# A ring of two buffers for the modulation's dots, and converted weights in four buffers instead of five

## The chip, the cores and the metric

The kernel runs on one core of one Trainium2 chip. The metric is the device time of one execution in microseconds, the median of several runs. The engines are named as in the profile: PE is TensorE (matmuls), PEld its weight loads, DVE is VectorE, ACT is ScalarE, POOL is GpSimd, and SP is the engine that issues most DMAs.

## The reference

Two layers of a decoder trunk, over 512 positions of 1024 features, in float32. Each layer is

```
mod = silu(c) @ w_ada + b_ada                 # six vectors of 1024: sh1, sc1, g1, sh2, sc2, g2
h = rmsnorm(x, norm1_w) * (1 + sc1) + sh1
u = h @ w_in                                  # pooling, convolution, q, k, v, gate logits
merged = sum of sigmoid(gate_i) * (mixer_i(u) @ p_i) over pooling, convolution, attention
x = x + g1 * (merged @ w_out)
h2 = rmsnorm(x, norm2_w) * (1 + sc2) + sh2
x = x + g2 * ((silu(h2 @ w_gate) * (h2 @ w_up)) @ w_down)
```

The vectors of `mod` depend on `c` alone, not on `x`; each can be made at any time before its use.

## The kernel before

**Numbers.** [...] Each operand is split in a high part (`whi` for weights) and a low part (`wlo`, the rest), and `mm3` adds high×high, high×low and low×high.

**Weights.** They come in 312 chunks of up to eight blocks of 128 × 128, in the order in which PE uses them. A chunk goes through three steps. SP fetches it (`fetch`, L232) into one of three `raw` buffers. ACT copies it to `whi` (L325, in `split_w`). DVE subtracts to get `wlo` (L328). `whi` and `wlo` have five buffers each, so the copy of a chunk waits until PE has ended the last matmul on the chunk that is five earlier. `next_w` (L349) asks for as many chunks as `ahead_now` says to be on their way beyond the one that it hands out: 4 in most phases, 3 in the gates' phase, and 2 in the last columns of the phases with a norm behind them, where the call gives the number itself. [...] The DVE part may also be held behind a step of the norm (`hold`).

In the gate and up projections most columns are done in pairs by a scheme that saves products and needs sums of weights (`Sums`, `GateUp`, `glu_pair`). There a chunk may be a sum, which POOL's DMAs (L254, L256) and DVE (L262, L263) make in tiles of the ring `w4`. Such a pair has seven chunks, with 256 columns to a matmul.

**The modulation.** A vector of 1024 takes eight dots. A dot (`ada_dot`, L374) is one DVE instruction over 128 × 1024 numbers that multiplies a piece of `w_ada` by silu(c) and adds up. Its piece is 512 KB, fetched by SP (L398) right where the dot is written down. The first 16 dots, for the first norm, are done at the start. The other 80 are made in steps (`ada_step`) as tasks in a queue `bulk`. PE's work calls `tick` every few matmuls, which adds `bulk_rate` to a credit of at most 4.0 and runs tasks until it is spent; a dot costs 1.2. So up to four dots are written down together when a phase begins with full credit. They are made in these places:

- the gates' phase, beside attention, which is written as generators and interleaved by hand: G1, SC2, SH2 in layer 0 and SC2, SH2 in layer 1 (L901), with `early=True`, so their pieces take a `raw` buffer
- the output projection: G2 (L1004), in `w4`, which has six buffers
- layer 0's first down projection: SC1 and SH1 of layer 1 (L1126), in `w4`
- layer 1's input projection: G1 (L849), in `w4`

Of the kernel before, what the change touches and what calls it, by code (L numbers as in the profile page):

```python
# [12 lines left out]
F32 = mybir.dt.float32  # L13
F32R = mybir.dt.float32r
# [7 lines left out]
P = 128  # L22
D = 1024
# [18 lines left out]
C_BLOCKS = 8  # L42
# [8 lines left out]
RAW, BIG = 3, 46  # L51
# [6 lines left out]
SH1, SC1, G1, SH2, SC2, G2 = range(6)  # L58
# [19 lines left out]
def hybrid_trunk(ctx, tc, xT, ws, ada, cols, pool_w, qk_w, crow, pos, con, out):  # L78
# [5 lines left out]
    wp = ctx.enter_context(tc.tile_pool(name="wp", bufs=4))  # L84
# [6 lines left out]
    def nm(s):  # L91
        uid[0] += 1
        return f"{s}{uid[0]}"
# [13 lines left out]
    def w4(shape, dt=F32):  # L107
        return work.tile(shape, dt, tag="w4", name=nm("w4"), bufs=6)
# [10 lines left out]
    bulk = deque()  # L119
# [31 lines left out]
    def pin(ins):  # L151
        return tc.keep_in_program_order(ins)
# [85 lines left out]
    class Sums:  # L238
# [19 lines left out]
        def first(self):  # L258
            raw = rawt()
            fetch(raw, self.l, self.blocks(0, 0) + self.blocks(1, 0))  # L260
            flat = raw.rearrange("p (g b) n -> p g (b n)", g=2)
            pin(V.tensor_add(self.s12[:, 1], self.s12[:, 0], flat[:, 0]))  # L262
            pin(V.tensor_add(self.s43[:, 0], self.s12[:, 1], flat[:, 1]))  # L263
            return split_w(raw, C_BLOCKS)

        def sums(self, which):
            t = (self.s12, self.s43)[which]
            return split_w(t.rearrange("p g (b n) -> p (g b) n", n=P), C_BLOCKS)

    class GateUp:  # L270
# [9 lines left out]
        def load(self, sub):  # L280
            if sub < 2:
                return self.pair[sub].first()
            if sub < 6:
                return self.pair[sub % 2].sums(sub // 2 - 1)
            raw = rawt()
            fetch(raw, self.l, self.pair[0].blocks(1, 1) + self.pair[1].blocks(1, 1))
            return split_w(raw, C_BLOCKS)
# [33 lines left out]
        return wp.tile([P, C_BLOCKS, P], F32, tag="raw", name=nm("raw"), bufs=RAW)  # L321

    def split_w(raw, n):
        hi = wp.tile([P, C_BLOCKS, P], F32R, tag="whi", name=nm("whi"), bufs=5)
        A.activation(hi[:, :n], raw[:, :n], AF.Copy)  # L325
        lo = wp.tile([P, C_BLOCKS, P], F32R, tag="wlo", name=nm("wlo"), bufs=5)
        with tc.issue_after(hold[0].ins) if hold[0] is not None else nullcontext():
            ins = V.tensor_sub(lo[:, :n], raw[:, :n], f32(hi)[:, :n])  # L328
        pin(ins)
        return hi, lo  # L330
# [13 lines left out]
        fetch(raw, l, blocks)  # L344
        return split_w(raw, len(blocks))

    ahead_now = [4]

    def next_w(ahead=None):  # L349
        ahead = ahead_now[0] if ahead is None else ahead  # L350
# [21 lines left out]
    def ada_dot(aw, l, part, j):  # L372

        return V.scalar_tensor_tensor(aw, aw, 1.0, csil, op0=ALU.mult, op1=ALU.mult,  # L374
                                      accum_out=mod[l][:, part, j:j + 1])
# [17 lines left out]
        else:  # L393
            A.activation(m, m, AF.Identity, bias=colt[:, 0, C_ADA + part * KT + j:C_ADA + part * KT + j + 1])

    def ada_step(l, part, j, early):
        aw = wp.tile([P, D], F32, tag="raw", name=nm("raw"), bufs=RAW) if early else w4([P, D])
        nc.sync.dma_start(aw, ada[l, part, j])  # L398
        pin(ada_dot(aw, l, part, j))

    def ada_end(l, part):
        m = mod[l][:, part]
        V.tensor_add(m, m, colt[:, l, C_ADA + part * KT:C_ADA + (part + 1) * KT])
        if part in (SC1, SC2):
            fold_scale(l, 0 if part == SC1 else 1, 0, KT)
        if part == G1:
            V.tensor_scalar(m, m, 0.5, None, op0=ALU.mult)

    def ada_tasks(l, parts, early=False):
        out = []  # L410
        for part in parts:
            for j in range(KT):
                out.append((1.2, lambda part=part, j=j: ada_step(l, part, j, early)))
            out.append((0.2, lambda part=part: ada_end(l, part)))
        return out

# [298 lines left out]
    for l in range(L):  # L715
# [118 lines left out]
        for j in range(2):  # L834
# [11 lines left out]
            if j == 1:  # L846
                bulk.append((0, lambda: pool_chain(1, pool1)))

        gains = ada_tasks(l, (G1,)) if l > 0 else []  # L849
        bulk.extend(gains[:4])  # L850
        k_ps = wide()
# [46 lines left out]
        V.tensor_mul(cv[1], pb, cv[1])  # L898
        y_conv.append(split_from(cv[1]))

        bulk.extend(ada_tasks(l, (G1, SC2, SH2)[l:], True))  # L901
        bulk_rate[0] = (0.5, 0.35)[l]
        ahead_now[0] = 3

        def gate():
            g = ps_mm()
# [93 lines left out]
                    hold[0] = nrm.apply(ll, i, k, lo, hi)  # L1000
            return go

        ahead_now[0] = 4
        bulk.extend(ada_tasks(l, (G2,)))  # L1004
        bulk_rate[0] = 0.9
        n2 = Norm()
# [241 lines left out]
```

## Time and profile before

| | |
|---|---|
| median of 3 runs | 1481.39 us (1480.77 to 1481.45) |
| profiled execution | 1480.46 us, span 1478.7 us |
| granted PE clock | 0.999 |
| PE busy | 1456.7 us, 99% |
| DVE busy | 1052.2 us, 71% |
| ACT busy | 666.3 us, 45% |
| dots in `w4` buffers | 56, 1220 ns each |
| dots in `raw` buffers | 40, 1218 ns each |

The 56 include the 16 first ones. The span runs from the first to the last instruction; the rest of an execution's time lies around it. In a row of the timeline stand the start and the duration in us, the engine, the line, the operation, what it writes and reads, how many instructions the row holds, and in brackets the idle time ahead and what ended it. In a row of the waits stand the total in us, the number and the longest.

### The profile page before, as it was taken

The page shows a single profiled execution, that of the slowest core. Times are in us where ns is not written, and L with a number is a line of the kernel's source. Part 1 is how long each engine was busy: PE and PEld are TensorE (multiplying, and loading weights), DVE is VectorE, ACT ScalarE, POOL GpSimd, SP SyncE. Part 2 cuts the span into 40 slices and gives each one's busy share as a digit, 9 for nine tenths or more (in the row PEclk, how much of TensorE's full clock was granted, in tenths as well). Part 3 has the DMA queues.
Part 4 walks back from the last instruction along what each step waited for, and adds up shares of the span by engine and source line. Part 5 has one row for each costly group of instructions (what it writes and reads, how often), then busy time and mean ns, then how long its engine had stood idle before and what let it go on. Part 6 is the DMA issues. An engine that isn't in the chain of part 4 may idle for free.

```text
span 1478.7 us, 21940 instructions
## 1 busy us (share of the span) xinstructions
PE 1456.7 (99%) x8443; PEld 1268.0 (86%) x8443; DVE 1052.2 (71%) x1855; ACT 666.3 (45%) x1138; POOL 105.8 (7%) x157
## 2 busy tenths in 40 slices
PE   8999999999999999999999999999999999999999
PEld 6888787778988998989988877778889889989997
DVE  7976887758686876767666777776586757657672
ACT  4634555443453352535444345455335525434350
POOL 0000000001100211210000000000010102111200
PEclk9999999999999999999999999999999999999999
DMA  9514433365337775744334443333462436637431
GB/s 346 199 73 159 141 136 134 115 227 148 109 114 221 207 190 174 198 113 117 114 109 146 155 143 126 102 114 128 143 193 81 141 114 167 191 89 196 131 105 65
DMA packets 84409, 217.19 MB, mean 147 GB/s; under 512 B 10832, under 2 KB 23760, under 8 KB 84304
## 3 DMA queue, kind: packets, MB, share of 16 engines
q1 hardware_dynamic: 67456, 177.37, 35.2%
q0 software_dynamic: 16128, 37.76, 11.6%
q8 instruction: 66, 1.08, 0.3%
q10 hardware_dynamic: 720, 0.66, 0.1%
q14 instruction: 39, 0.32, 0.1%
HBM read 213.65 MB, written 2.10 MB: 146 GB/s over the span
## 4 chain that ended last, share of the span: by engine, by line
PE 84%; DVE 8%; DMA 3%; ACT 3%; issue 1%; SPq 0%; DVEq 0%; ACTq 0%
PE mm L149 72%; PE pair L149 11%; DMA raw<-in_ws 2%; DVE wlo L328 2%; PE mm L155 1%; ACT whi L325 1%; DMA w<-in_ada 1%; DVE w L374 1%; DVE raw L374 1%; ACT tmp L612 0%; DMA x<-in_xT 0%; ACT tmp L614 0%; DVE big L914 0%; SPq L232 0%; DVE big L929 0%
## 5 line engine op out<-in xcount | busy, mean ns | idle before, releaser
L149 PE MATMUL mm<-big,whi 128*128 128x512 f32 (+1 forms) x4362 | 1083.3, 340 | 5.6 <-DVE tmp L1081 2.5
L149 PEld LDWEIGHTS mm<-big,whi 128*128 128x128 f32 x4362 | 746.0, 190 | 93.6 <-DVE tmp L1081 4.1
L149 PE MATMUL mm<-big,wlo 128*128 128x512 f32 (+1 forms) x2181 | 736.1, 337 | 0.0
L149 PEld LDWEIGHTS mm<-big,wlo 128*128 128x128 f32 x2181 | 413.9, 190 | 44.7
L325 ACT ACTIVATE whi<-raw 128x1024 fp32r<-128x1024 f32 (+2 forms) x240 | 248.8, 1039 | 298.3 <-PE mm L149 231.1
L328 DVE TENSOR_TENSOR wlo<-raw,whi 128x1024 fp32r<-128x1024 f32 (+2 forms) x240 | 284.7, 1193 | 81.9 <-ACT whi L325 81.0
L325 ACT ACTIVATE whi<-w 128x1024 fp32r<-128x1024 f32 x72 | 76.2, 1059 | 147.8 <-PE mm L149 107.7
L954 DVE SCALAR_TENSOR_TENSOR x<-mm,mod,x 128x512 f32<-128x512 f32 (+1 forms) x90 | 62.0, 689 | 101.4 <-PE mm L149 101.3
L254 POOL DMA_DIRECT2D w<-in_ws x72 | 48.5, 683 | 982.1 <-DVE w L374 377.3
L328 DVE TENSOR_TENSOR wlo<-w,whi 128x1024 fp32r<-128x1024 f32 x72 | 86.7, 1220 | 31.0 <-ACT whi L325 30.2
L149 PE MATMUL pair<-whi,big 128*128 128x512 f32 x224 | 76.7, 390 | 0.0
L256 POOL DMA_DIRECT2D w<-in_ws x72 | 64.6, 923 | 153.1 <-DMA w<-in_ws 136.3
L149 PE MATMUL pair<-big,whi 128*128 128x256 f32 (+1 forms) x376 | 74.0, 294 | 0.0
L374 DVE SCALAR_TENSOR_TENSOR w<-w,csil 128x1024 f32<-128x1024 f32 x56 | 66.9, 1220 | 9.5 <-DMA w<-in_ada 9.3
L149 PEld LDWEIGHTS pair<-big,whi 128*128 128x128 f32 x376 | 60.4, 191 | 2.2
L149 PE MATMUL mm<-whi,big 128*128 128x512 f32 x160 | 57.2, 394 | 1.7 <-ACT big L497 1.4
L149 PE MATMUL pair<-big,wlo 128*128 128x256 f32 (+1 forms) x188 | 55.3, 294 | 0.0
L511 DVE TENSOR_TENSOR big<-tmp,big 128x512 fp32r<-128x512 f32 x48 | 33.0, 690 | 24.3 <-ACT big L510 23.4
L149 PEld LDWEIGHTS pair<-whi,big 128*128 128x128 f32 x224 | 42.1, 188 | 8.7
L374 DVE SCALAR_TENSOR_TENSOR raw<-raw,csil 128x1024 f32<-128x1024 f32 x40 | 48.4, 1218 | 1.2 <-DMA raw<-in_ada 1.2
L914 DVE SCALAR_TENSOR_TENSOR big<-big,mm 128x512 f32<-128x512 f32 x48 | 32.6, 682 | 21.5 <-PE mm L149 21.1
L149 PE MATMUL pair<-wlo,big 128*128 128x512 f32 x112 | 43.6, 390 | 0.0
(187 smaller groups left out, 1251.5 us busy)
## 6 DMA issues: line engine op xcount, KB each, us to landing
raw<-in_ws SPq DMA_DIRECT2D x146, 512.0 KB, 3.4
w<-in_ws POOLq DMA_DIRECT2D x144, 256.0 KB, 4.6
w<-in_ada SPq DMA_DIRECT2D x56, 512.0 KB, 5.3
raw<-in_ada SPq DMA_DIRECT2D x40, 512.0 KB, 3.2
raw<-in_ws SPq DMA_DIRECT2D x64, 256.0 KB, 4.2
raw<-in_ws SPq DMA_DIRECT2D x24, 384.0 KB, 3.5
raw<-in_ws SPq DMA_DIRECT2D x16, 448.0 KB, 5.3
raw<-in_ws SPq DMA_DIRECT2D x36, 128.0 KB, 3.0
```

The costliest lines, as they stand in the source:

```text
L149: tc.keep_in_program_order(T.matmul(*a, **k))
L155: tc.keep_in_program_order(T.transpose(*a))
L254: nc.gpsimd.dma_start(dst, self.source(0, 1))
L256: nc.gpsimd.dma_start(dst, self.source(*other), accum_op=ALU.add)
L325: A.activation(hi[:, :n], raw[:, :n], AF.Copy)
L328: ins = V.tensor_sub(lo[:, :n], raw[:, :n], f32(hi)[:, :n])
L374: return V.scalar_tensor_tensor(aw, aw, 1.0, csil, op0=ALU.mult, op1=ALU.mult, accum_out=mod[l][:, part, j:j + 1])
L511: V.tensor_sub(lo, src, f32(hi))
L914: V.scalar_tensor_tensor(sg, sg, 1.0, branch, op0=ALU.add, op1=ALU.mult)
L954: V.scalar_tensor_tensor(x[k][:, lo:hi], src, mod[l][:, part, k:k + 1], x[k][:, lo:hi], op0=ALU.mult, op1=ALU.add)
```

## The change

Three things change together. The room in memory stays the same to the byte: two dot tiles of 4 KB a partition come, and one `whi` and one `wlo` of 4 KB each go.

1. `whi` and `wlo` have four buffers instead of five.
2. `ahead_now` is one less in every phase: 3 instead of 4, and 2 instead of 3 in the gates' phase. The calls of `next_w` that give the number themselves stay.
3. A dot's piece goes to a ring `dot` with two buffers that nothing else uses, in all four places; `early` goes. The fetch of a dot now waits for the dot that is two earlier, and no longer for a weight's conversion or a sum.

```
     def split_w(raw, n):
-        hi = wp.tile([P, C_BLOCKS, P], F32R, tag="whi", name=nm("whi"), bufs=5)
+        hi = wp.tile([P, C_BLOCKS, P], F32R, tag="whi", name=nm("whi"), bufs=4)
         A.activation(hi[:, :n], raw[:, :n], AF.Copy)
-        lo = wp.tile([P, C_BLOCKS, P], F32R, tag="wlo", name=nm("wlo"), bufs=5)
+        lo = wp.tile([P, C_BLOCKS, P], F32R, tag="wlo", name=nm("wlo"), bufs=4)
...
-    ahead_now = [4]
+    ahead_now = [3]
...
-    def ada_step(l, part, j, early):
-        aw = wp.tile([P, D], F32, tag="raw", name=nm("raw"), bufs=RAW) if early else w4([P, D])
+    def ada_step(l, part, j):
+        aw = wp.tile([P, D], F32, tag="dot", name=nm("dot"), bufs=2)
         nc.sync.dma_start(aw, ada[l, part, j])
         pin(ada_dot(aw, l, part, j))
...
-        bulk.extend(ada_tasks(l, (G1, SC2, SH2)[l:], True))
+        bulk.extend(ada_tasks(l, (G1, SC2, SH2)[l:]))
         bulk_rate[0] = (0.5, 0.35)[l]
-        ahead_now[0] = 3
+        ahead_now[0] = 2
...
-        ahead_now[0] = 4
+        ahead_now[0] = 3
         bulk.extend(ada_tasks(l, (G2,)))
         bulk_rate[0] = 0.9
```

The order of PE's instructions is the same in both kernels; on ACT, DVE and SP some conversions, dots and fetches change places.

More of the change, by code (lines that the diff above doesn't have):

```diff
@@ L407, in ada_end, with ada_tasks @@
             V.tensor_scalar(m, m, 0.5, None, op0=ALU.mult)
-    def ada_tasks(l, parts, early=False):
+    def ada_tasks(l, parts):
         out = []
@@ L412, in ada_tasks @@
             for j in range(KT):
-                out.append((1.2, lambda part=part, j=j: ada_step(l, part, j, early)))
+                out.append((1.2, lambda part=part, j=j: ada_step(l, part, j)))
             out.append((0.2, lambda part=part: ada_end(l, part)))
```

## The prediction

> **What bounds the kernel now.** I read the page first, then the waits of TensorE alone, then those of ScalarE (ACT), and at the end the timeline around the places where the modulation's dots run.
>
> ```profile
> span 1478.7 us, 21940 instructions
> ...
> PE 1456.7 (99%) x8443; PEld 1268.0 (86%) x8443; DVE 1052.2 (71%) x1855; ACT 666.3 (45%) x1138; POOL 105.8 (7%) x157
> ...
> w<-in_ada SPq DMA_DIRECT2D x56, 512.0 KB, 5.3
> raw<-in_ada SPq DMA_DIRECT2D x40, 512.0 KB, 3.2
> ```
>
> PE is busy 1456.7 of 1478.7 us, so at most 22 us are idle, and the start of the program has a part of that. The next view lists what TensorE waits for.
>
> ```profile
> PE mm L155 <- DVE tmp L619: 4.7, 5, 1.9
> PE mm L149 <- DVE tmp L1081: 2.5, 8, 0.6
> PE mm L149 <- ACT big L909: 2.4, 1, 2.4
> ```
>
> Columns: total us, number, longest. These are the top three rows. No row of this view names a converted weight (`whi` of L325 or `wlo` of L328): TensorE never waits for weights. The largest rows belong to attention (softmax at L619, the gate's branch at L909). The span can therefore fall only through attention's rows, 4.7 + 2.4 = 7.1 us, and grow wherever a conversion, today early, becomes late.
>
> ```profile
> ACT whi L325 <- PE mm L149: 338.8, 141, 4.6
> ACT whi L325 <- DMA raw<-in_ws: 40.1, 27, 3.8
> ```
>
> These are the first two rows of ACT's waits. The first is the lead: 141 conversions wait until TensorE has finished with the buffer they are to overwrite. The kernel runs as far ahead as its buffers allow. The second is the fault that the dots bring: a weight that has not landed yet, with ACT standing in order behind it.
>
> **The change, part by part.** No work goes or comes: the same conversions, the same 80 dots that are made in steps, the same DMAs. What moves is when each may start.
>
> *One buffer fewer, one chunk less ahead.* In phases 512 columns wide, a chunk of eight blocks is 24 matmuls.
>
> ```profile
> 411.70 0.62 PE L149 MATMUL pair<-big,whi 128*128 128x512 f32 x2
> ...
> 412.38 0.62 PE L149 MATMUL mm<-big,whi 128*128 128x512 f32 x2
> ```
>
> Three matmuls take 412.38 − 411.70 = 0.68 us, so a chunk takes 24 × 0.227 = 5.45 us, and the lead of a conversion falls from four chunks (21.8 us) to three (16.3 us). ACT's and DVE's part of one chunk is under 3 us together (two rows of about 1.06 and 1.22 us, shown below), so I cost this at 0 in the wide phases, from 0 to 0. In the gate/up pairs a matmul has 256 columns:
>
> ```profile
> 490.52 1.22 DVE L328 TENSOR_TENSOR wlo<-raw,whi 128x1024 fp32r<-128x1024 f32 x1
> ...
> 498.45 1.23 DVE L328 TENSOR_TENSOR wlo<-w,whi 128x1024 fp32r<-128x1024 f32 x1 [1.18 <-ACT whi L325]
> ```
>
> ```profile
> 492.92 0.40 PE L149 MATMUL pair<-big,whi 128*128 128x256 f32 x2
> ...
> 494.35 0.40 PE L149 MATMUL pair<-big,whi 128*128 128x256 f32 x2
> ...
> 505.87 0.40 PE L149 MATMUL mm<-big,whi 128*128 128x256 f32 x2
> ```
>
> The first fence is DVE, the second PE. From 492.92 to 494.35 lie 12 matmuls, 0.12 us each, so a chunk is 2.88 us. The `wlo` that ends at 499.68 is first used at 505.87, a slack of 6.2 us, which falls by one chunk (2.9) to 3.3: still no wait, so I take 0 in the steady pairs. The upper end is a slack used up in every one of the 18 pairs (72 sums at four a pair), by 0.3 us each, +5.4; I leave that to a rival. The first pair is tighter: the `wlo` that starts at 490.52 ends at 491.74 and is used at 494.35, 2.6 us. That place is costed with the dots.
>
> In the second norm the same cut moves one `wlo` out of the row of three that DVE does just ahead of the norm's apply, to the place of the next row:
>
> ```profile
> 411.55 2.69 DVE L328 TENSOR_TENSOR wlo<-raw,whi 128x768 fp32r<-128x768 f32 x3
> ...
> 401.82 0.39 PE L149 MATMUL mm<-big,whi 128*128 128x256 f32 x1 [0.19 <-DVE big L484]
> ```
>
> One such `wlo` is 2.69 / 3 = 0.90 us. Without it DVE is 0.9 us earlier at L484, and the wait of 0.19 us at 401.82 goes. In exchange that `wlo` ends at 411.55 + 0.90 = 412.45, while TensorE wants its chunk at 412.38: 0.07 late. Twice in the program: −0.2 us, from −0.4 to +0.6.
>
> *Dots out of the raw ring.* Weights and dots share three raw buffers in the gates' phase today, and SP sends both in order.
>
> ```profile
> 845.72 23.18 SPq L398 DMA_DIRECT2D raw<-in_ada  x4
> 869.73 0.33 SPq L232 DMA_DIRECT2D raw<-in_ws  x1
> ```
>
> ```profile
> 243.00 1.06 ACT L325 ACTIVATE whi<-raw 128x1024 fp32r<-128x1024 f32 x1 [1.02 <-DMA raw<-in_ws]
> ...
> 938.75 1.06 ACT L325 ACTIVATE whi<-raw 128x1024 fp32r<-128x1024 f32 x1 [3.77 <-DMA raw<-in_ws]
> ```
>
> ```profile
> 247.36 0.85 PE L155 MATMUL mm<-ident,tmp 128*128 128x128 f32 x6 [0.42 <-DVE tmp L619]
> ...
> 943.12 1.65 PE L149 MATMUL mm<-w,big 128*128 128x256 f32 x6 [2.36 <-ACT big L909]
> ```
>
> Four fetches of dots keep SP from 845.72 to 868.90, and the weight behind them goes out at 869.73. Later in the phase ACT stands 3.77 us at a `whi` whose weight hasn't landed, then runs softmax's exponentials and L909, and TensorE has waited 2.36 us for L909. With dots in their own ring the weights have all three raw buffers and are fetched about a chunk earlier: the ACT wait goes. What is late next is softmax's own chain and the transposes that L909's neighbours read, so not all 2.36 come back: −1.2. ACT's wait of 1.02 us ahead of the stall at 247.36 gives no more than the 0.42 that TensorE waited there: −0.4. Of the other waits for L619, 4.7 − 0.4 = 4.3 us, I take a tenth, since ACT's waits near them are short or none: −0.4. Together −2.0, from 0 to −7.1 (all of attention's rows).
>
> *Two dots at a time instead of three or six.* This is the added wait. When a phase begins, the credit lets four dots into DVE's order at once. DVE is in order: whatever is queued behind a dot waits for that dot's DMA.
>
> ```profile
> 857.26 1.21 DVE L328 TENSOR_TENSOR wlo<-raw,whi 128x1024 fp32r<-128x1024 f32 x1
> ...
> 867.32 1.22 DVE L374 SCALAR_TENSOR_TENSOR raw<-raw,csil 128x1024 f32<-128x1024 f32 x1
> ```
>
> ```profile
> 875.98 0.63 PE L149 MATMUL mm<-big,whi 128*128 128x512 f32 x2
> ```
>
> Today three dots run back to back from 867.32, none waiting for its fetch. After, the third and fourth fetch can go only when the first two dots have ended, at 868.5 and 869.6 (867.32 + 1.15, + 2.3). With the landing times of the page, 3.2 to 5.3 us, the fourth dot starts between 872.9 and 875 and ends 1.2 later. The `wlo` that runs at 857.26 today, 18.7 us before its use at 875.98, goes to the place behind the fourth dot, since it needs a buffer one chunk later. It would end between 875.3 and 877.5. That, and softmax pieces (L619) queued behind the same dots, give +1.2 us, from 0 to +2.5. The same burst in layer 0 has no weight due behind it: +0.3, from 0 to +1.
>
> The third place is layer 0's first down projection, where 16 dots for the next layer's first norm are made, eight in this stretch, two in the time of 18 matmuls of 512 columns (6 × 0.68 = 4.08 us). Today up to six of their fetches are out together.
>
> ```profile
> 470.81 12.71 SPq L398 DMA_DIRECT2D w<-in_ada  x6
> ```
>
> ```profile
> 485.04 1.21 DVE L328 TENSOR_TENSOR wlo<-raw,whi 128x1024 fp32r<-128x1024 f32 x1
> ```
>
> With two buffers a buffer's cycle is landing (3.2 to 5.3) plus the dot (1.2) plus issue: 4.6 to 6.7 us for each two dots against 4.08 wanted. Over four such steps the last dots are 2 to 10 us later. Besides, SP's order puts a weight fetch, which waits for a `wlo` that now stands behind the dots, ahead of the last two dots' fetches. Behind those dots on DVE stand two additions of a pair's sums and two `wlo`: today at 485.04 and 490.52, wanted by TensorE at 492.92 and 494.35. A delay of 6 us would make the first end at 485.04 + 6 + 1.2 = 492.3, in time, and the second, which follows it by 5.5 us today but by about 3.5 when pressed, end near 497: +2.0 us, from 0 to +5. The dots for G2 in the two output projections lie in a wide phase with 16 us of lead: 0.
>
> [...]
>
> *Sum.* 0 + 0 − 0.2 − 2.0 + 1.2 + 0.3 + 2.0 + 0 = +1.3 us. The profiled execution took 1480.46 us (1478.7 in the span, 1.8 around it); it lies 0.9 under the median of the runs, 1481.39, so I add the sum to the median: 1482.7 us.
>
> **The rivals.**
>
> *Attention gains and the dots are hidden.* For it: 40.1 us of ACT's waiting is for weights behind dots, and TensorE waits in attention only behind ACT and DVE. If about two thirds of the 7.1 us come back (−4.7) and dots cost nothing, with −0.2 from the norms: 1476.5 us. Against it: L619's row has causes of its own, and of its five waits only the first has been matched with a late weight.
>
> *The dots' ring of two holds DVE.* Place: the stretch from 470 to 498 and its sibling at the gates of layer 1. It decides when a dot's fetch lands more than 4.08 − 1.2 = 2.9 us after issue, which both rows of the page say, and when the last `wlo` is pushed past 494.35. At the upper ends, +5 and +2.5 and +1, with −1.0 gained in attention: +7.5, some 1488 to 1489 us. Against it: with only two fetches out, landing may be nearer 3.2 than 5.3.
>
> *The shorter lead shows in the pairs.* The slack of 6.2 us is that of one row; if DVE's order uses it up, 18 pairs by 0.3 us are +5.4, with the sum +6.7: 1488 us. Against it: 3.3 us are left.
>
> *Nothing changes.* TensorE is 99% busy and waits for no weight; SP's fetches were hidden and still are. Then 1481.4 us.
>
> **How the numbers follow.** Forecast 0.42; the ring holds DVE 0.20; attention gains 0.16; nothing changes 0.14; the pairs 0.08. A measurement of this kernel can tell about 0.2%, 3.0 us, from no change. Faster by more: the attention rival and a small edge of the forecast, 0.17. Slower by more: the two slow rivals and the upper edge of the forecast, 0.34. Between: 0.49. The forecast's own range, by its terms' likelier ends, is 1479.5 to 1485.5; the range that holds 8 in 10 takes in the attention rival in part and the slow rivals up to their price: 1477.5 to 1488.5.
>
> **What would show it right or wrong.** Right: ACT's wait for `raw<-in_ws` falls from 40.1 us to well below 25; the TensorE wait of 2.36 us at L909 shrinks; DVE's row of dots waiting for their DMA grows to some tens of us; a new TensorE wait for `wlo` of L328 (or ACT's `whi`) of 2 us at about 493 to 498, and of 1 us at about 876. Wrong: no row of L328 or L325 in TensorE's waits (then the dots are hidden), or such rows all through the gate/up pairs (then the lead is what counts), or attention's rows 4.7 and 2.4 unchanged while ACT's wait has gone (then the raw ring was never their cause).

## The result and the profile after

Timed side by side, 20 executions each, the changed kernel took 1482.63 us (median; 1480.77 to 1486.93) and the kernel before 1479.77 us (1476.64 to 1483.36). The ratio is 1.0022, with a 95% interval of 1.0013 to 1.0031: slower, by 2.9 us (0.2%). On another chip the same comparison (12 and 30 executions) gave 1.0012 (1.0000 to 1.0024). The profiled execution of the changed kernel took 1486.59 us, one of its slowest, so its trace shows more loss than the median has; a second profile, of 1482.40 us, is used beside it.

The page of the changed kernel, engines and the dots' fetches:

```profile
span 1484.8 us, 21967 instructions
...
PE 1460.9 (98%) x8443; PEld 1269.0 (85%) x8443; DVE 1050.8 (71%) x1855; ACT 662.0 (45%) x1138; POOL 106.9 (7%) x157
...
dot<-in_ada SPq DMA_DIRECT2D x80, 512.0 KB, 4.1
```

PE has the same 8443 matmuls and 4.2 us more busy time, which is not work: the first matmul behind a wait is shown longer (0.39 us instead of 0.28 in the pair below), and some ran at a lower clock (0.69 from 632.40 to 636.60, below). What PE waits for (total, times, longest):

```profile
PE mm L149 <- DVE tmp L1081: 5.9, 18, 0.4
PE mm L155 <- DVE tmp L619: 3.6, 4, 1.2
PE mm L149 <- ACT big L510: 1.3, 1, 1.3
...
PE pair L149 <- DVE wlo L328: 1.1, 1, 1.1
...
PE mm L149 <- ACT big L909: 0.5, 1, 0.5
...
PE mm L149 <- DVE wlo L328: 0.3, 1, 0.3
```

The row of L1081 has gone from 2.5 us and 8 times to 5.9 us and 18 times: it is now in every one of the 18 gate/up pairs, once. Attention's rows went from 4.7 and 2.4 to 3.6 and 0.5. The two rows of `wlo` are new. From all engines' waits, the raw weights that ACT waits for, and the dots that DVE waits for:

```profile
DVE dot L374 <- DMA dot<-in_ada: 22.6, 23, 2.6
...
ACT whi L325 <- DMA raw<-in_ws: 17.6, 11, 3.3
```

PE's matmuls come in the same order in both kernels, so the start of the same matmul can be subtracted, after minus before, and followed through the program:

| up to | before | after | difference |
|---|---|---|---|
| start done | 18.14 | 18.00 | −0.14 |
| end of layer 0's attention | 303.94 | 301.90 | −2.04 |
| second norm of layer 0 | 401.82 | 399.71 | −2.11 |
| first pair behind the dots | 494.59 | 493.79 | −0.80 |
| start of layer 0's third down projection | 630.22 | 632.50 | +2.28 |
| twelve matmuls later | 633.57 | 637.45 | +3.88 |
| last pair of layer 0 that did not wait before | 689.48 | 694.53 | +5.05 |
| burst of dots in layer 1 | 876.45 | 881.92 | +5.47 |
| L909's reader | 943.12 | 946.98 | +3.86 |
| ten matmuls later | 946.26 | 948.73 | +2.47 |
| second norm of layer 1 | 1132.39 | 1135.36 | +2.97 |
| last pair of layer 1 that did not wait before | 1419.54 | 1425.94 | +6.40 |

In the second profile the same column runs −1.90 at the end of layer 0's attention, −2.00 at its second norm, +1.59 in the row of layer 0's last pair, −1.06 behind L909's slow matmuls and +2.23 in the last row. In both profiles attention gave 4.2 us net: 1.9 in layer 0, and in layer 1 3.0 at L909's reader, of which 0.8 was lost again in the 75 us behind it. In both the pairs took 5.9. What the first profile lost beyond the second lies at the first pair (1.3 us) and at the start of the third down projection: +2.5 there, from one wait of 1.32 us for L510 and a clock of 0.69 over the 4.2 us behind it, against −0.4 in the second.

**The pairs.** One of them on DVE, in the kernel before, then in the changed kernel, then PE in the changed kernel:

```profile
508.88 0.69 DVE L1090 TENSOR_TENSOR tmp<-tmp,tmp 128x512 f32<-128x512 f32 x1 [0.37 <-ACT tmp L1087]
509.49 0.41 DVE L1081 TENSOR_TENSOR tmp<-tmp,mm 128x256 f32<-128x256 f32 x1
509.98 1.23 DVE L328 TENSOR_TENSOR wlo<-w,whi 128x1024 fp32r<-128x1024 f32 x1
511.12 0.41 DVE L1081 TENSOR_TENSOR tmp<-tmp,mm 128x256 f32<-128x256 f32 x1
```

```profile
508.00 0.69 DVE L263 TENSOR_TENSOR w<-w,raw 128x512 f32<-128x512 f32 x1
508.60 0.42 DVE L1077 TENSOR_TENSOR tmp<-tmp,mm 128x256 f32<-128x256 f32 x1
508.93 0.41 DVE L1081 TENSOR_TENSOR tmp<-tmp,mm 128x256 f32<-128x256 f32 x1
509.26 0.69 DVE L1090 TENSOR_TENSOR tmp<-tmp,tmp 128x512 f32<-128x512 f32 x1
509.87 1.22 DVE L328 TENSOR_TENSOR wlo<-raw,whi 128x1024 fp32r<-128x1024 f32 x1
511.00 0.42 DVE L1081 TENSOR_TENSOR tmp<-tmp,mm 128x256 f32<-128x256 f32 x1
```

```profile
510.81 0.28 PE L149 MATMUL mm<-big,wlo 128*128 128x256 f32 x1
511.47 0.39 PE L149 MATMUL mm<-big,whi 128*128 128x256 f32 x1 [0.38 <-DVE tmp L1081]
```

L1081 adds a partial product out of the PSUM tile that PE's next group goes on adding to, so that group waits for it. In both kernels a `wlo` of 1.2 us stands between the two additions on DVE. Before, PE's work just covered this. After, the sums of a pair (L262, L263) run just ahead of the additions, and the product L1090, which ran ahead of both additions before, stands between them with the `wlo`. PE, which could go on behind the matmul of 510.81, is ready some 0.5 us ahead of DVE, and waits. No weight is late there.

What stands between the two additions on DVE tells, pair by pair, whether PE waits:

| kernel | in ten pairs | in the other eight | pairs in which PE waits |
|---|---|---|---|
| before | `wlo` | L511 and `wlo` | the eight |
| changed, both profiles; the lead alone | L1090 and `wlo` | L511 and `wlo` | all 18 |
| the order alone; every run with the later load | nothing | L511 | none |

In the ten the matmul behind the wait and the few after it move by 0.59 us each, 5.9 us in all; in the eight that waited before they do not get later. So the order on DVE is not simply the one in which the program was written down: L1090 is written behind both additions. `pin` is what keeps an instruction at its written place.

**The first pair behind the dots**, DVE and then PE:

```profile
488.86 1.22 DVE L328 TENSOR_TENSOR wlo<-raw,whi 128x1024 fp32r<-128x1024 f32 x1
...
492.51 1.22 DVE L328 TENSOR_TENSOR wlo<-raw,whi 128x1024 fp32r<-128x1024 f32 x1
```

```profile
493.79 0.39 PE L149 MATMUL pair<-big,wlo 128*128 128x256 f32 x1 [1.14 <-DVE wlo L328]
```

The two `wlo` that ran at 485.04 and 490.52 run at 488.86 and 492.51, and PE, which is 2.1 us earlier here than before, waits 1.14 us for the second. In the second profile there is no such wait: the place is at its edge.

**Attention in layer 1.** PE at L909's reader, and PE's granted clock (the third figure from the end) in the 3.1 us behind it in the kernel before:

```profile
946.98 0.98 PE L149 MATMUL mm<-w,big 128*128 128x256 f32 x6 [0.54 <-ACT big L909]
```

```profile
943.10:946.20 3.10, 3.08 (x10) 2.77 (x11) 3.10 (x6) 0.92 (x2) 0.00 (x0) 0.50 0.03 12
```

Before, the wait of 2.36 us was followed by 3.1 us at a clock of 0.50. After, PE waits 0.54 us and the clock is 1.00 from 943 to 950. The place gave 5.47 − 2.47 = 3.0 us, not 1.2.

### The profile page after: what moved, and what is told of

It is laid out like the page before. It is cut to its first block, busy times and chain, and to the rows that moved or that the text cites. A ratio compares the mean times of both kernels' runs of the same rounds, so it can differ in the third digit from the quotient of the medians.

```text
span 1484.8 us, 21967 instructions
## 1 busy us (share of the span) xinstructions
PE 1460.9 (98%) x8443; PEld 1269.0 (85%) x8443; DVE 1050.8 (71%) x1855; ACT 662.0 (45%) x1138; POOL 106.9 (7%) x157
## 5 line engine op out<-in xcount | busy, mean ns | idle before, releaser
L374 DVE SCALAR_TENSOR_TENSOR dot<-dot,csil 128x1024 f32<-128x1024 f32 x80 | 97.2, 1222 | 22.9 <-DMA dot<-in_ada 22.6
L511 DVE TENSOR_TENSOR big<-tmp,big 128x512 fp32r<-128x512 f32 x48 | 32.9, 692 | 29.9 <-ACT big L510 28.9
L630 ACT ACTIVATE w<-mm 128x512 fp32r<-128x512 f32 (+2 forms) x48 | 24.0, 525 | 33.4 <-PE mm L155 33.2
```

The costliest lines, as they stand in the source:

```text
L511: V.tensor_sub(lo, src, f32(hi))
L630: A.activation(both[:, :, :, 0], tp, AF.Copy)
```

## The experiments

The kernel before ran beside every experiment; its medians lay between 1480.69 and 1481.31 us.

**The lead alone.**

```
whi, wlo: bufs 5 -> 4;  ahead_now 4/3 -> 3/2;  dots stay in raw and w4
```

> Four buffers for converted weights and one chunk less ahead, but the dots stay in the raw and w4 rings as in the kernel before. Theory A (the shorter lead costs): in each gate/up pair DVE's second L1081 comes too late and TensorE waits about 0.6 us, some eleven times, +6 to +7 us against the kernel before, and attention gains nothing (ACT's wait for raw weights stays near 40 us). Theory B (the ring of two dots costs): within 1.5 us of the kernel before, the L1081 row near 2.5 us.

1488.42 us, ratio 1.0048 (1.0031 to 1.0065), +7.1 us. PE's and ACT's waits:

```profile
PE mm L149 <- DVE tmp L1081: 5.9, 18, 0.4
```

```profile
ACT whi L325 <- DMA raw<-in_ws: 45.0, 30, 4.2
```

The shorter lead costs 7.1 us, and the ring of dots, which is the rest of the change, gives 1488.42 − 1482.85 = 5.6 us (the changed kernel beside it). Theory A holds, and B, that the ring is what costs, falls. The waits are 18, not eleven: eight of them were there before.

**The order alone.**

```
ahead_now 4/3 -> 3/2;  five buffers and the dots as before
```

> Five buffers and the dots as in the kernel before; only one chunk less ahead. Theory A1 (it is the place in DVE's order that counts, set by the lead): the same loss as with four buffers, +6 to +7 us. Theory A2 (it is the release of the buffer by TensorE that sets when a conversion starts): less than 2 us of loss, the L1081 row near 2.5 us.

1481.83 us, ratio 1.0004 (0.9992 to 1.0016). PE has no row for L1081 at all; DVE in one pair, then PE's first row and ACT's row for raw weights:

```profile
517.05 0.95 DVE L1081 TENSOR_TENSOR tmp<-tmp,mm 128x256 f32<-128x256 f32 x2
517.91 1.22 DVE L328 TENSOR_TENSOR wlo<-w,whi 128x1024 fp32r<-128x1024 f32 x1
```

```profile
PE mm L155 <- DVE tmp L619: 7.5, 9, 2.0
```

```profile
ACT whi L325 <- DMA raw<-in_ws: 102.3, 68, 4.5
```

With a fifth buffer both additions stand side by side, with no `wlo` between them in any pair, and A1 falls: the lead by itself does not put it there; four buffers with a lead of three do. A2 had the time right, but expected the row to stay near 2.5. Its reason, that PE's release of a buffer sets the time of a conversion, is not shown: from 500 to 690 us ACT's copies wait for PE 52.6 us in 23 waits here and 56.6 in 19 in the changed kernel. Why four buffers give the other order stays open. The time is no better than before: in this trace layer 0's attention ends 6.5 us later than before (in the changed kernel 2.0 earlier), which the pairs do not win back. ACT waited 102 us for raw weights instead of 40; the lead alone, with four buffers, the same calls and the same rings, waited 45, so the shorter lead is not the whole reason for that.

**The changed kernel again**, beside these two.

> The changed kernel itself, on the chip of the other three. Both theories: 2 to 5 us over the kernel before; TensorE's waits for L1081 again about 18 times and 6 us, attention's rows (L619 with L909) near 4 us, a wait for wlo of about 1.1 us at the first pair after the dots.

1482.85 us, ratio 1.0012 (1.0000 to 1.0024), +1.5 us, under the 2 to 5 that were expected. L1081 again 5.9 us in 18 waits; no row for `wlo`, against what was expected.

**The load later in the pairs.**

```
-            w = [next_w() for _ in both]          # ahead of B22
+            w = [next_w(), next_w(2)]
...
-                V.tensor_add(m22, m22, a[z])      # L1081
+                pin(V.tensor_add(m22, m22, a[z]))
```

> The changed kernel, where in each gate/up pair one chunk's load (its sums and its conversion) is written down behind the two additions of L1081 instead of ahead of them. Theory A: TensorE's row for L1081 goes from about 6 us to under 1.5, and the time falls by 5 to 7 us against the changed kernel, to 2 or 3 us under the kernel before. Theory B: no change against the changed kernel. A third possibility: the conversion is then itself too late, with a new TensorE row for wlo of L328 in every pair.

1480.07 us, 2.8 us under the changed kernel; against the kernel before 0.9989 (0.9975 to 1.0003). The edit has two parts, the call of `next_w` and the `pin` that keeps the additions in their place; no run took them apart. L1081 is gone from PE's waits, and no row for `wlo` came in the pairs, but the gain is half of what was expected. The row that grows is the copy at the start of the down projections, 0.4 us in one wait in the changed kernel beside it:

```profile
PE mm L149 <- ACT big L510: 3.2, 3, 1.2
```

**The same in the kernel before** (`next_w(3)` there).

> The kernel before with one edit: in each gate/up pair one chunk's load stands behind the two additions of L1081. If DVE's order around L1081 is the cause of that wait in both kernels, TensorE's row for L1081 (2.5 us in the waits, about 0.4 us a time with the weight load) goes to under 0.5 and the time falls by 2 to 4 us. If it is set by something else, nothing changes.

1477.73 us, ratio 0.9974 (0.9964 to 0.9985), −3.0 us, and no row for L1081. The order around L1081 cost the kernel before as well, in fewer pairs.

**Three buffers for dots.**

```
dot: bufs 2 -> 3;  w4: bufs 6 -> 5 (for the room)
```

> The changed kernel with three buffers for dots (and five instead of six in the w4 ring, to make room). If the two-deep ring costs TensorE 1 to 3 us, as the prediction's terms for the dots had it, DVE's wait for dots' DMAs falls from about 22 us to under 10 and the time falls by 1 to 2.5 us against the changed kernel. If the waits are hidden in most executions, the time stays within 1 us of it.

1500.80 us, ratio 1.0137 (1.0122 to 1.0153). DVE's wait for dots fell to 9.1 us, but the room was taken from the wrong place:

```profile
PE mm L149 <- DVE w L631: 14.6, 10, 2.2
```

L631 writes attention's probabilities into `w4`; with five buffers PE waits for them. What a third dot buffer is worth stays open.

**Five buffers with the dots' ring**, room from raw (3 to 2) and `w4` (6 to 5), `ahead_now` 3/2.

> Five buffers for converted weights, one chunk less ahead, dots in their ring of two; the room comes from two raw buffers instead of three and five w4 buffers instead of six. If buffer release is the cause of the pairs' loss and the dots' ring the cause of attention's gain, both show: no row for L1081, attention's rows near 4 us, and 5 to 8 us under the kernel before. Rival: two raw buffers are too few; then ACT's wait for raw weights goes over 60 us, and the time is at or above the kernel before.

1577.75 us, ratio 1.0648 (1.0630 to 1.0666). ACT waited 304.0 us for raw weights, PE 39.6 us for L1081 and 18.2 for L631. Two raw buffers are too few, as the rival had it; the pairing of five buffers with the ring wasn't settled.

**The later load with four raw buffers** (`w4` 6 to 5).

> The changed kernel with the later load in the pairs, four raw buffers instead of three and five w4 buffers instead of six. If the waits for L510 at the start of the down projections (3.2 us with the later load) come from raw fetches that go out too late, they fall under 1.5 us and the time is 2 us under the later load alone. If those fetches land late because other transfers share the time, nothing changes.

1492.94 us, ratio 1.0076 (1.0064 to 1.0088). L631 again, 15.0 us, hides the answer; L510 is no longer among PE's large rows, and ACT's wait for raw weights is 4.1 us.

**One buffer for dots.**

```
dot: bufs 2 -> 1
```

> The changed kernel with one buffer for dots instead of two. It shows what a dot's wait costs TensorE. If DVE, in order, is near its edge at the first pair and at the bursts, as the prediction's terms for the dots had it, DVE's wait for dots' DMAs at least doubles from 22 us, TensorE gets a row for wlo of L328 of 5 us or more, and the time rises by 5 to 15 us. If slack covers it, the time stays within 2 us of the changed kernel.

1512.24 us, ratio 1.0207 (1.0188 to 1.0226), some 30 us over the changed kernel; of which, from trace to trace, +11.8 arise at one matmul, 22 matmuls ahead of the first pair, and +7.0 at layer 1's burst. PE's first row, then DVE ahead of that matmul, which starts at 506.08:

```profile
PE mm L149 <- DVE wlo L328: 19.0, 2, 11.7
```

```profile
499.00 1.23 DVE L374 SCALAR_TENSOR_TENSOR dot<-dot,csil 128x1024 f32<-128x1024 f32 x1 [3.30 <-DMA dot<-in_ada]
...
503.65 1.23 DVE L374 SCALAR_TENSOR_TENSOR dot<-dot,csil 128x1024 f32<-128x1024 f32 x1 [3.42 <-DMA dot<-in_ada]
504.80 1.22 DVE L328 TENSOR_TENSOR wlo<-raw,whi 128x1024 fp32r<-128x1024 f32 x1
506.02 1.22 DVE L328 TENSOR_TENSOR wlo<-raw,whi 128x1024 fp32r<-128x1024 f32 x1
```

The dots stand 4.6 us apart, one fetch and one dot, and the conversion stands behind them. The mechanism that the prediction feared is real, behind the two bursts that it named, the first time one chunk earlier than it said; two buffers are just enough.

**Both kernels with the later load, and the down projection's third weight copy held behind L510.**

```
+            hold_hi[0] = last_split[0]     # behind the pairs
...
+        with tc.issue_after(hold_hi[0].ins) if hold_hi[0] is not None else nullcontext():
             A.activation(hi[:, :n], raw[:, :n], AF.Copy)
```

> The changed kernel with the later load in the pairs, and with the copy of the down projection's third chunk on ACT held behind the last L510 copy of the pairs. In the run with the later load alone TensorE waited 3.2 us for L510 behind a copy whose weight had not landed. Expected: that row falls under 1 us, and 2 to 4 us less than the later load alone, 3 to 5 us under the kernel before. Rival: the next thing is late instead, and the time stays as with the later load alone, 1 us under the kernel before.

> The kernel before with the same two edits (later load in the pairs, the down projection's copy held behind L510). The later load alone gave 3.0 us. The second edit has little to win here, as no L510 row was among the large ones: 2.5 to 4 us under the kernel before.

The changed kernel: 1476.54 us, ratio 0.9966 (0.9954 to 0.9979). The kernel before: 1477.24 us, 0.9971 (0.9959 to 0.9984). Both beat both kernels, and they cannot be told apart. For the kernel before the second edit brought nothing (0.9974 without it). In the changed one PE still waits 3.6 us, now two times, for the same copy (L514 there): the row did not fall as expected. ACT has no weight copy just ahead of L514 there. DVE, then ACT:

```profile
628.20 1.22 DVE L332 TENSOR_TENSOR wlo<-raw,whi 128x1024 fp32r<-128x1024 f32 x1 [3.37 <-ACT whi L328]
629.34 0.42 DVE L1096 SCALAR_TENSOR_TENSOR tmp<-tmp,tmp 128x256 f32<-128x256 f32 x1
629.67 0.42 DVE L1097 SCALAR_TENSOR_TENSOR tmp<-mm,tmp 128x256 f32<-128x256 f32 x1
```

```profile
630.12 0.63 ACT L514 ACTIVATE big<-tmp 128x512 fp32r<-128x512 f32 x1 [1.69 <-DVE tmp L1097]
```

L514 waits for L1097, and that stands on DVE behind a `wlo` whose weight came late. With the later load alone it was so too (L510 waited 0.66 us for L1093), so the copy that was held back was not the one in the way. What the total gained over the later load alone, 0.9966 against 0.9989 with intervals that touch, is not found in the traces.

**The lead alone with the later load.**

> Four buffers, one chunk less ahead, the dots in the rings of the kernel before (as in the run of the lead alone, +7.1 us), with the later load in the pairs. If all of the lead's loss sits at L1081, the row vanishes and the time is within 1.5 us of the kernel before, 6 to 8 us under the lead alone. If the lead also costs elsewhere (attention, the norms, the start of the down projections), it stays 2 us or more above the kernel before.

1485.49 us, ratio 1.0030 (1.0018 to 1.0041), +4.2 us, and L1081 is gone. So the shorter lead costs elsewhere too, at least with the later load: the row of L510 was 1.2 us in the lead alone. PE's first row; one of its three waits on ACT, on DVE and on PE; and the granted clock behind it (third figure from the end):

```profile
PE mm L149 <- ACT big L510: 4.7, 3, 2.2
```

```profile
627.98 1.06 ACT L325 ACTIVATE whi<-raw 128x1024 fp32r<-128x1024 f32 x1 [3.12 <-DMA raw<-in_ws]
...
631.00 0.63 ACT L510 ACTIVATE big<-tmp 128x512 fp32r<-128x512 f32 x1 [0.60 <-DVE tmp L1093]
```

```profile
629.08 1.22 DVE L328 TENSOR_TENSOR wlo<-raw,whi 128x1024 fp32r<-128x1024 f32 x1 [2.98 <-ACT whi L325]
630.22 0.42 DVE L1092 SCALAR_TENSOR_TENSOR tmp<-tmp,tmp 128x256 f32<-128x256 f32 x1
630.55 0.42 DVE L1093 SCALAR_TENSOR_TENSOR tmp<-mm,tmp 128x256 f32<-128x256 f32 x1
```

```profile
631.68 0.50 PE L149 MATMUL mm<-big,whi 128*128 128x512 f32 x1 [2.24 <-ACT big L510]
```

```profile
632.00:636.00 4.00, 3.77 (x10) 2.86 (x10) 2.18 (x3) 0.00 (x0) 0.00 (x0) 0.59 0.60 207
```

A weight lands late (ACT waits 3.12 us for it, 1.85 in the kernel before), and DVE stands at its `wlo`. Behind that in DVE's order stand L1092 and L1093; L510, which the down projection needs, waits for L1093. It is the mechanism of the pairs again: work stands behind a conversion. PE then pays twice: 2.24 us of waiting, and a clock of 0.59 over the next 4 us.

## Why the prediction was right, and where it was not

The total was right: 1482.7 us forecast, 1482.63 measured, and the forecast's sum of +1.3 us lies just under the interval of +1.9 to +4.6 of the first comparison (20 executions each) and inside that of the second. The agreement is luck, twice over. The change cost 2.9 us, 1.6 more than the sum, and the median of three runs to which the sum was added, 1481.39, lies 1.6 above the later one of 20. And the sum itself is near because its errors cancel: in the second profile the pairs cost 5.9 us that it had at nothing, attention gave 2.2 us more than it had, and the dots, 3.5 in the sum, cost under 1. Of the signs that it named, ACT's wait, L909 and DVE's waits for dots came; the waits for `wlo` came at both places but smaller, and at the first pair in one profile of two.

- *Wide phases, 0*: right. No conversion was awaited there.
- *Steady pairs, 0*: this step failed; it was +5.9. It measured the slack from a `wlo` to the matmul that reads it, 6.2 us, which was right and not what counts. What a conversion delays is what stands behind it on DVE, and there stood L1081, a row that the prediction had quoted (2.5 us, 8 times) and not followed. In ten more pairs it now came too late, by 0.59 us each. The rival of the pairs had about the right price, +5.4, for the wrong reason: no weight was late.
- *The start of the down projections* was in no term. The prediction saw no cost of a later raw fetch there. In the changed kernel it cost 2.5 us in one profile and nothing in the other. With the later load it is the largest row that the shorter lead adds (4.7 us without the ring of dots, 3.2 with it).
- *Second norms, −0.2*: right in sign, and somewhat larger: the program moved by −0.16 us across the one of layer 0 and by −0.40 across the one of layer 1.
- *Attention, −2.0*: right in its mechanism, too small in size. ACT's wait for raw weights fell from 40.1 to 17.6 us, L909's wait from 2.36 to 0.54, and 4.2 us net came back: 1.9 in layer 0, most of it at waits for softmax (L619), and 3.0 less 0.8 in layer 1. What was missing is the clock of 0.50 over the 3.1 us behind the wait for L909, which cost some 1.4 us, and one wait for L619 of 1.87 us at 303.94, which fell to under half and of which the sum had taken a tenth.
- *Bursts, +1.2 and +0.3*: too large in layer 1 (+0.4 in the second profile). The fourth dot and the `wlo` behind it came as forecast (it ended at 881.86, between the bounds once the 5.5 us that the program is late there are taken off), and PE waited 0.33 us.
- *First pair, +2.0*: the two `wlo` were late by 3.8 and 2.0 us, as the order said, for +1.3 us in one profile and 0 in the other. One buffer instead of two made it 12 us, one chunk earlier, which shows the mechanism.
- *The rival of attention* had about the right gain (−4.7) and the wrong company; *the ring holds DVE* decided nothing at two buffers.

Whether the ring of dots is a loss depends on its buffers. At one buffer it is (53.4 us of DVE waiting for dots, +30 us). At two it is not: 22.6 us of waiting on DVE, and the ring gives 5.6 us.

## What to carry to other kernels

When a producer gets less lead, do not ask only whether its product is still in time: read which other instructions stand behind it on its engine, and who waits for those. Rows that are just in time, such as an addition that ends 0.1 us ahead of the matmul that needs it, are where the next half microsecond will show, and they repeat as often as the loop. Moving one load behind two additions was worth as much, 3.0 us, as the whole change cost.

## What the runs showed of the hardware

Some waits of PE of 1.3 to 2.4 us were followed by a lower granted clock: 0.50 over the 3.1 us behind the 2.36 us at 943.12 before, 0.59 over the 4 us behind 2.24 us with the lead alone and the later load, and 0.69 over the 4.2 us behind 1.32 us in the changed kernel:

```profile
632.40:636.60 4.20, 3.88 (x10) 2.84 (x11) 2.49 (x3) 0.05 (x1) 0.00 (x0) 0.69 0.29 103
```

So each cost more than its own length, by about 1.5 us. That is an estimate from the clock that these three stretches lacked: 3.1 × 0.50 = 1.55, 4 × 0.41 = 1.64 and 4.2 × 0.31 = 1.30 us.

The wait of 1.87 us at 303.94 in the kernel before, longer than those 1.32 us, was not followed by a lower clock: it was 1.00 from 303.90 to 308.00. So in these traces the length of a wait alone does not tell whether the clock falls behind it. What else decides stays open.
